# A new end for a decoder layer: gathered tokens settled per column group, folded part by products at the very end

## The chip, the cores and the metric

One NeuronCore of a Trainium2 chip. The metric is device time in microseconds (us) of one execution. TensorE (PE), VectorE (DVE), ScalarE (ACT), GpSimd (POOL) and SyncE (SP) each work through a list of instructions of their own, in order, and wait for each other by semaphores.

## What is computed

A decoder layer on 512 tokens of 2048 columns: a mixer, then an expert network (PEER) that picks 128 of 16384 single-neuron experts for every token. Only the end of the expert part is touched:

```
def apply(args):
    xb, ib, gb = args
    u = jnp.take(expert_u, ib, axis=0)
    a = jnp.einsum('thkd,td->thk', u, xb)
    w = (jax.nn.gelu(a.astype(jnp.float32), approximate=False) * gb).astype(xb.dtype)
    vv = jnp.take(expert_v, ib, axis=0)
    return jnp.einsum('thk,thkd->td', w, vv)
...
x = x + gate2[:, None, :] * ffn
```

All in float32.

## The kernel before

Of the 512 tokens, 352 are **dense**: every expert is computed for them, by products over all 16384 rows of `expert_u` and `expert_v`, with weights that are zero where an expert was not picked. The other 160 are **gathered**: the rows of their picked experts are fetched by indirect DMAs from POOL, and DVE multiplies and adds. The gathered tokens come in two groups: the first has 128 tokens, one on each partition. The second has 32 tokens, each of them on four partitions that hold a quarter of its experts each; its sum has to be folded, four partitions into one.

*Dense part.* The experts go in 16 chunks of 8 blocks of 128. For a chunk, `u_block` (L790) makes the activations of each block, `w_block` makes from them the weights `W`, and `v_group(ch, dg)` multiplies them with `expert_v` for four column groups `dg` of 512 columns (L943). Weights come by SP's queue (`vr`, L933, three buffers), and are split in two halves of fewer bits each (`split`, L88 on ACT for the upper half, L89 on DVE for the lower one); three products of 128x128 by 128x352 then stand for one of float32. A group of a chunk takes four loads of two blocks, each with 24 products: 96 products a group, 384 a chunk. In the last chunk the result of a group does not go to `acc`, but to `xs[dg]`: x from DRAM (`begin`, L966) plus `acc` times the gate (L970), plus the last chunk's sums times the gate (L951). `xs[dg]` is kept transposed: 128 columns on the partitions, tokens along the free dimension; tokens 0 to 127 are the first gathered group, 128 to 159 the second, 160 to 511 the dense ones.

*Gathered part.* `gathered` fetches 128 half rows of 1024 columns by one indirect DMA (L842, four buffers `gt`), and DVE adds each, times its weight, to `gacc` (L867). When the first group's sum is finished it goes to DRAM (`a_dram`), and the second group uses `gacc` again. In the last chunk all steps left are written into the program at once (`gather_to(NK)`), before the four calls of `v_group`; the last gathers are those of the second group's `expert_v`.

*The end.* In the last chunk `add_gathered(dg)` follows `v_group(dg)`, and `store` follows one group later (`ADD_AT`, `STORE_AT`). `add_gathered` loads the group's columns of `a_dram` (L976), transposes four blocks of them (L982) and four blocks of `gacc` (L986), copies both by ACT (L984, L987), folds the second by three additions on DVE each (L989), and corrects `xs` by both at once (L991). `store` transposes a whole group back, four tiles of 128 tokens (L1000), copies each (`ot`, L1003 on DVE, L1005 on ACT), and sends it to `out` (L1006).

*What sets the order.* The engines' lists are made by a scheduler of the framework, from the order of the source and an estimate of its own; so calls that follow each other in the source are interleaved. PSUM holds two buffers `pa` for transposes and three double buffers `pv`, which the sums of a group (two of them) and the transposes of `store` share.

Of the kernel before, what the change touches and what calls it, by code (L numbers as in the profile page):

```python
# [22 lines left out]
P = 128  # L23
# [23 lines left out]
ADD_AT = ((0,), (1,), (2,), (3,))  # L47
STORE_AT = ((), (0,), (1,), (2, 3))
# [30 lines left out]
def hymba_peer(tc, x, c, positions, w_ada, b_ada, norm1_g, w_in, conv_w, q_norm_g, k_norm_g,  # L79
# [18 lines left out]
    with ExitStack() as ctx:  # L98
# [9 lines left out]
        make_identity(nc, ident)  # L108
        modc = const.tile([P, 6, KC], F32, name="modc")
# [863 lines left out]
        def add_gathered(dg):  # L973
            if NG == 2:
                ar = fin.tile([P, 512], F32, name="ar")
                nc.sync.dma_start(ar, a_dram[:, dg * 512:(dg + 1) * 512])  # L976
            else:
                ar = gacc[:, dg * 512:(dg + 1) * 512]
            for j in range(4):
                k = dg * 4 + j  # L980
                pt = psA.tile([P, T], F32, name="pa").rearrange("p (j t) -> p j t", t=P)
                nc.tensor.transpose(pt[:, 0], ar[:, j * P:(j + 1) * P], ident)  # L982
                ft = fin.tile([P, TG], F32, name="ft")
                nc.scalar.activation(ft[:, 0:P], pt[:, 0], AF.Copy)  # L984
                if NG == 2:
                    nc.tensor.transpose(pt[:, 1], gacc[:, k * P:(k + 1) * P], ident)  # L986
                    nc.scalar.activation(ft[:, P:], pt[:, 1, 0:nb], AF.Copy)  # L987
                    for f in range(1, fold):
                        nc.vector.tensor_tensor(out=ft[:, P:], in0=ft[:, P:],  # L989
                                                in1=pt[:, 1, f * nb:(f + 1) * nb], op=OP.add)  # L990
                nc.vector.scalar_tensor_tensor(xs[dg][:, j, 0:TG], ft, modc[:, 5, k:k + 1], xs[dg][:, j, 0:TG],  # L991
                                               op0=OP.mult, op1=OP.add)

        def store(dg):
            for i in range(NT):
                if i % 2 == 0:
                    pq = psV.tile([P, 2, T], F32, name="pv")
                po = pq[:, i % 2]
# [3 lines left out]
                if i % 2:  # L1002
                    nc.vector.tensor_copy(ot, po)  # L1003
                else:
                    nc.scalar.activation(ot, po, AF.Copy)  # L1005
                nc.sync.dma_start(out[i * P:(i + 1) * P, dg * 512:(dg + 1) * 512], ot)  # L1006

# [45 lines left out]
```

## Time and profile before

| | us |
|---|---|
| median of 3 runs | 3570.03 |
| lowest, highest | 3550.63, 3575.09 |
| profiled execution | 3566.93 |
| its span, first to last instruction | 3565.0 |
| PE busy (share of the span) | 3243.3 (91%) |
| DVE busy | 2853.7 (80%) |
| POOL busy | 1403.5 (39%) |
| ACT busy | 1222.7 (34%) |

Times in the rows below are us from the span's start unless marked ns. A row of the timeline merges instructions of one kind that follow each other (`x44`); in brackets stands how long the engine had been idle before it, and what ended that. PEclk is the granted clock of TensorE as a share of 2.4 GHz. DMA is the mean busy share of the 16 DMA engines.

### The profile page before, as it was taken

The numbers are of one execution on the slowest core, as the hardware profiler recorded it, in microseconds if no ns is written. First come the engines' busy times: TensorE is split into PE (matmuls) and PEld (weight loads), VectorE is DVE, ScalarE is ACT, GpSimd is POOL, SyncE is SP. The second block draws the span as 40 slices with busy tenths as digits, with TensorE's granted clock in tenths as the row PEclk, the third lists the DMA queues.
The fourth block names the chain that finished last, engine by engine and source line by source line (L and its number), as shares of the span: only waits on it lengthen the run. The fifth ranks groups of instructions, "written<-read, shape, count | busy, mean of one in ns | idle before, by whom it ended". The sixth has DMA issues, their size and how long they took to land.

```text
span 3565.0 us, 48376 instructions
## 1 busy us (share of the span) xinstructions
PE 3243.3 (91%) x18006; PEld 2980.4 (84%) x18006; DVE 2853.7 (80%) x4261; ACT 1222.7 (34%) x1828; POOL 1403.5 (39%) x985
## 2 busy tenths in 40 slices
PE   5988999999998797899999989899999999999986
PEld 4766777777787696899899989899999999989985
DVE  5789776743369989778888888898988999988985
ACT  5232333342264357322232222233322233223222
POOL 2446332254346410135444343343343444334441
PEclk9999999999999899999999999999999999999998
DMA  8864755559722135899999999999999999999994
GB/s 284 284 226 149 253 192 182 183 167 314 219 74 79 60 141 190 245 302 303 300 305 303 290 306 312 299 297 301 306 305 301 292 315 312 303 291 295 298 304 171
DMA packets 417514, 896.26 MB, mean 251 GB/s; under 512 B 32209, under 2 KB 110974, under 8 KB 412542
## 3 DMA queue, kind: packets, MB, share of 16 engines
q1 hardware_dynamic: 325118, 557.59, 53.5%
q0 software_dynamic: 92160, 335.59, 27.8%
q8 instruction: 141, 2.31, 0.3%
q14 instruction: 95, 0.78, 0.1%
HBM read 843.47 MB, written 49.55 MB: 250 GB/s over the span
## 4 chain that ended last, share of the span: by engine, by line
DMA 39%; DVE 28%; PE 16%; issue 11%; POOL 3%; ACT 1%; SPq 1%; DVEq 0%; POOLq 0%; ACTq 0%
DMA gt<-in_expert_v_dram,idxu 10%; DMA gt<-in_expert_u_dram,idxu 7%; DMA vr<-in_expert_v_dram 4%; PE pm L457 4%; DMA ada_w<-in_w_ada_dram 4%; POOL gt L842 3%; DVE gacc L867 3%; DMA gt<-in_expert_v_dram,ib 3%; DVE ada_acc L196 2%; DMA ur<-in_expert_u_dram 2%; DVE utf L778 2%; DVE gt L851 2%; DMA gt<-in_expert_u_dram,ib 2%; DVE gt L905 2%; DVE vs L89 2%
## 5 line engine op out<-in xcount | busy, mean ns | idle before, releaser
L790 PE MATMUL pa<-hd,ut 128*128 128x352 f32 x6144 | 1084.3, 329 | 69.4 <-DVE ut L89 59.8
L943 PE MATMUL pv<-W,vs 128*128 128x352 f32 x6144 | 1081.3, 329 | 71.6 <-DVE vs L89 42.8
L943 PEld LDWEIGHTS pv<-W,vs 128*128 128x128 f32 x6144 | 1017.6, 192 | 89.5 <-DVE vs L89 54.0
L790 PEld LDWEIGHTS pa<-hd,ut 128*128 128x128 f32 x6144 | 1020.4, 192 | 82.2 <-DVE ut L89 70.1
L89 POOL TENSOR_TENSOR wsp<-wraw,wsp 128x1024 fp32r<-128x1024 f32 x160 | 392.8, 2457 | 565.5 <-ACT wsp L88 536.2
L842 POOL DMA_INDIRECT gt<-in_expert_u_dram,idxu x256 | 344.1, 1344 | 636.3 <-DVE gt L851 307.2
L88 ACT ACTIVATE vs<-vr 128x1024 fp32r<-128x1024 f32 x256 | 271.2, 1059 | 813.8 <-PE pv L943 384.8
L842 POOL DMA_INDIRECT gt<-in_expert_v_dram,idxu x256 | 329.2, 1286 | 493.4 <-DVE gacc L867 333.7
L867 DVE SCALAR_TENSOR_TENSOR gacc<-gt,ga_a,gacc 128x1024 f32<-128x1024 f32 x316 | 400.1, 1275 | 106.9 <-DMA gt<-in_expert_v_dram,idxu 74.9
L851 DVE SCALAR_TENSOR_TENSOR gt<-gt,h2n 128x1024 f32<-128x1024 f32 x320 | 385.5, 1216 | 123.3 <-DMA gt<-in_expert_u_dram,idxu 99.7
L88 ACT ACTIVATE ut<-utf 128x1024 fp32r<-128x1024 f32 x232 | 244.6, 1056 | 284.6 <-DVE utf L778 158.5
L89 DVE TENSOR_TENSOR vs<-vr,vs 128x1024 fp32r<-128x1024 f32 x256 | 309.2, 1209 | 37.2 <-ACT vs L88 37.2
L778 DVE STREAM_TRANSPOSE utf<-ur 128x1024 f32<-128x1024 f32 x232 | 286.7, 1237 | 6.7 <-issue 3.3
L88 ACT ACTIVATE wsp<-wraw 128x1024 fp32r<-128x1024 f32 x160 | 169.1, 1058 | 355.7 <-issue 94.1
L89 DVE TENSOR_TENSOR ut<-utf,ut 128x1024 fp32r<-128x1024 f32 x232 | 281.5, 1215 | 9.7 <-ACT ut L88 9.7
L457 PE MATMUL pm<-big,wsp 128*128 128x512 f32 x1152 | 285.6, 400 | 0.0
L457 PEld LDWEIGHTS pm<-big,wsp 128*128 128x128 f32 x1152 | 213.9, 191 | 42.2
L196 DVE SCALAR_TENSOR_TENSOR ada_acc<-ada_w,scol,ada_acc 128x512 f32<-128x512 f32 x195 | 211.5, 1085 | 28.0 <-DMA ada_w<-in_w_ada_dram 24.3
L245 PE MATMUL pqk<-wsp,big 128*128 128x512 f32 x768 | 193.1, 411 | 18.8 <-DVE qk L291 11.4
L699 PE MATMUL pm<-big,wsp 128*128 128x512 f32 x768 | 187.8, 402 | 17.0 <-POOL wsp L89 15.4
L245 PEld LDWEIGHTS pqk<-wsp,big 128*128 128x128 f32 x768 | 150.0, 198 | 55.5 <-DVE qk L291 14.2
L545 PE MATMUL pm<-big,wsp 128*128 128x512 f32 x768 | 182.7, 398 | 8.4 <-DVE x L551 8.4
(274 smaller groups left out, 3167.6 us busy)
## 6 DMA issues: line engine op xcount, KB each, us to landing
vr<-in_expert_v_dram SPq DMA_DIRECT2D x256, 512.0 KB
ur<-in_expert_u_dram SPq DMA_DIRECT2D x464, 256.0 KB
ada_w<-in_w_ada_dram SPq DMA_DIRECT2D x192, 512.0 KB
wraw<-in_w_in_dram SPq DMA_DIRECT2D x96, 512.0 KB
g_dram<-gtile SPq DMA_DIRECT2D x11, 2048.0 KB
g<-g_dram SPq DMA_DIRECT2D x32, 704.0 KB
wraw<-in_w_out_dram SPq DMA_DIRECT2D x32, 512.0 KB
wraw<-in_w_peer_q_dram SPq DMA_DIRECT2D x32, 512.0 KB
```

The source lines that it names most:

```text
L88: hi = nc.scalar.activation(dst[:, 0], src, AF.Copy)
L89: (eng or nc.vector).tensor_tensor(out=dst[:, 1], in0=src, in1=dst[:, 0].bitcast(F32), op=OP.subtract)
L196: nc.vector.scalar_tensor_tensor(new, wt[:, k], s, old, op0=OP.mult, op1=OP.add)
L245: nc.tensor.matmul(banks[i], hT[kk][:, a, i * P:(i + 1) * P], ws[:, b, k], start=(kk == last[0] and n == 0), stop=(kk == last[1] and n == 2))
L457: nc.tensor.matmul(banks[n2], ws[:, a, k, n2 * P:(n2 + 1) * P], hT[kk][:, b], start=(kk == 0 and n == 0), stop=(kk == KC - 1 and n == 2))
L699: nc.tensor.matmul(banks[j], ws[:, a, k, j * P:(j + 1) * P], h2T[kk][:, b], start=(kk == 0 and n == 0), stop=(kk == KC - 1 and n == 2))
L778: nc.vector.transpose(t, UR[0][:, :, q * 256:(q + 1) * 256].rearrange("p b (c r) -> p c b r", r=32))
L790: mm = nc.tensor.matmul(pa[:, :TD], ut[:, a, j], hd[k][:, b], start=(k == 0 and n == 0), stop=(k == KC - 1 and n == 2))
L842: d = nc.gpsimd.indirect_dma_start(out=t, out_offset=None, in_=src, in_offset=bass.IndirectOffsetOnAxis(ap=gidx[g][:, j:j + 1], axis=0), e ...
L851: nc.vector.scalar_tensor_tensor(t, t, 1.0, h2n[:, f * D // 2:(f + 1) * D // 2], op0=OP.mult, op1=OP.mult, accum_out=ga_a[:, f, j:j + 1])
L867: nc.vector.scalar_tensor_tensor(gacc[:, s], t, a, gacc[:, s], op0=OP.mult, op1=OP.add)
L943: mm = nc.tensor.matmul(pv[j // 2][:, j % 2, :TD], vs[:, a, bb, j * P:(j + 1) * P], W[e0 // 2][:, m, bb], start=(b == 0 and n == 0), stop= ...
```

## The change

`add_gathered` and `store(dg)` go; three functions come. `settle(dg)`, called one group late, corrects the tokens of the first gathered group alone, straight from PSUM (L996), and stores the three tiles that hold none of the second group's tokens: tiles 2, 3 and 0. `settle_last` follows everything: sixteen products of `gacc` with a 128x32 matrix of ones and zeros (`foldm`, made at the start from the identity by one DVE reduction) transpose and fold at once (L1004); one multiplication by the gate (L1007), an addition to each group (L1010), and tile 1 of each group is stored. The products are held behind the dense ones by an order without a wait.

```
-ADD_AT = ((0,), (1,), (2,), (3,))
-STORE_AT = ((), (0,), (1,), (2, 3))
...
+        foldm = const.tile([P, TG - P], F32, name="foldm")
+        nc.vector.tensor_reduce(foldm, ident.rearrange("p (f t) -> p t f", t=TG - P), axis=AX.X, op=OP.add)
...
-        def add_gathered(dg):
...
+        def store(dg, tiles):
+            for n, i in enumerate(tiles):
+                if n % 2 == 0:
                     pq = psV.tile([P, 2, T], F32, name="pv")
+                po = pq[:, n % 2]
...
+                if (n + dg) % 2:
                     nc.vector.tensor_copy(ot, po)
                 else:
                     nc.scalar.activation(ot, po, AF.Copy)
                 nc.sync.dma_start(out[i * P:(i + 1) * P, dg * 512:(dg + 1) * 512], ot)
+
+        def settle(dg):
+            ar = fin.tile([P, 512], F32, name="ar")
+            nc.sync.dma_start(ar, a_dram[:, dg * 512:(dg + 1) * 512])
+            pt = psA.tile([P, T], F32, name="pa").rearrange("p (j t) -> p j t", t=P)
+            for j in range(4):
+                nc.tensor.transpose(pt[:, j], ar[:, j * P:(j + 1) * P], ident)
+            for j in range(4):
+                k = dg * 4 + j
+                nc.vector.scalar_tensor_tensor(xs[dg][:, j, 0:P], pt[:, j], modc[:, 5, k:k + 1], xs[dg][:, j, 0:P],
+                                               op0=OP.mult, op1=OP.add)
+            store(dg, (2, 3, 0))
+
+        def settle_last():
+            pt = psA.tile([P, T], F32, name="pa").rearrange("p (k t) -> p k t", t=nb)
+            for k in range(KC):
+                mm = nc.tensor.matmul(pt[:, k], gacc[:, k * P:(k + 1) * P], foldm, start=True, stop=True)
+                tc.add_manual_dep(mm.ins, pace[-1].ins.name, ORDER, reason="products of the dense tokens first")
+            ft = fin.tile([P, KC, nb], F32, name="ft", bufs=1)
+            nc.vector.tensor_tensor(out=ft, in0=pt, in1=modc[:, 5, :, None].to_broadcast([P, KC, nb]), op=OP.mult)
+            for dg in range(4):
+                x_ = xs[dg][:, :, P:TG]
+                nc.vector.tensor_tensor(out=x_, in0=x_, in1=ft[:, dg * 4:dg * 4 + 4], op=OP.add)
+                store(dg, (1,))
...
-                if ch == nch - 1:
-                    for f in ADD_AT[dg]:
-                        add_gathered(f)
-                    for f in STORE_AT[dg]:
-                        store(f)
+                if ch == nch - 1 and dg:
+                    settle(dg - 1)
+        settle(3)
+        settle_last()
```

Line numbers of the split are two lower after the change (L86, L87). Up to the products of the last chunk the engines' lists are otherwise the same.

PE's list, from the last product of the first column group on, before the change (`pv` are the sums, `ar` the first gathered group, `gacc` the second, `xs` what is stored):

```order
L943 MATMUL pv<-W,vs 128x352 x36
L982 MATMUL pa<-ident,ar 128x128 x2
L943 MATMUL pv<-W,vs 128x352 x84
L986 MATMUL pa<-ident,gacc 128x128 x2
L982 MATMUL pa<-ident,ar 128x128 x2
L1000 MATMUL pv<-ident,xs 128x128 x5
L943 MATMUL pv<-W,vs 128x352 x14
```

and after it:

```order
L943 MATMUL pv<-W,vs 128x352 x52
L993 MATMUL pa<-ident,ar 128x128 x4
L943 MATMUL pv<-W,vs 128x352 x20
L979 MATMUL pv<-ident,xs 128x128 x2
L943 MATMUL pv<-W,vs 128x352 x4
L979 MATMUL pv<-ident,xs 128x128 x2
L993 MATMUL pa<-ident,ar 128x128 x4
L943 MATMUL pv<-W,vs 128x352 x24
L979 MATMUL pv<-ident,xs 128x128 x4
L993 MATMUL pa<-ident,ar 128x128 x4
L943 MATMUL pv<-W,vs 128x352 x20
L979 MATMUL pv<-ident,xs 128x128 x4
```

The transposes of `gacc` (L986), which stood behind 84 products of the second group and ahead of the 192 of the third and fourth, are gone from this place; transposes of stored tiles (L979) stand there, tile 0 last. The end of PE's list after the change:

```order
L943 MATMUL pv<-W,vs 128x352 x20
L1004 MATMUL pa<-foldm,gacc 128x32 x7
L979 MATMUL pv<-ident,xs 128x128
L1004 MATMUL pa<-foldm,gacc 128x32
L979 MATMUL pv<-ident,xs 128x128 x5
L1004 MATMUL pa<-foldm,gacc 128x32 x2
L979 MATMUL pv<-ident,xs 128x128
```

The products with `foldm` follow the last dense product, with transposes of the last group's tiles among them; 28 transposes of stored tiles stand behind the last dense product.

DVE's list before, from the second group's x on (`vs` is a split, `gacc` a gathered row added):

```order
L970 SCALAR_TENSOR_TENSOR xs<-acc,modc,xs 128x352 x4
L867 SCALAR_TENSOR_TENSOR gacc<-gt,ga_a,gacc 128x1024 x7
L989 TENSOR_TENSOR ft<-ft,pa 128x32 x6
L991 SCALAR_TENSOR_TENSOR xs<-ft,modc,xs 128x160 x2
```

These rows close the gathers before the change, with six splits still behind them. After the change, from the copy of a stored tile of the first group on:

```order
L867 SCALAR_TENSOR_TENSOR gacc<-gt,ga_a,gacc 128x1024 x2
L982 COPY ot<-pv 128x512
L87 TENSOR_TENSOR vs<-vr,vs 128x1024
L951 SCALAR_TENSOR_TENSOR xs<-pv,modc,xs 128x352 x4
L970 SCALAR_TENSOR_TENSOR xs<-acc,modc,xs 128x352 x4
L996 SCALAR_TENSOR_TENSOR xs<-pa,modc,xs 128x128 x4
L87 TENSOR_TENSOR vs<-vr,vs 128x1024
L867 SCALAR_TENSOR_TENSOR gacc<-gt,ga_a,gacc 128x1024 x2
L982 COPY ot<-pv 128x512
L87 TENSOR_TENSOR vs<-vr,vs 128x1024
```

The last gathers are spread between splits, copies and corrections, and reach to two splits before the end of the dense part. On SP six stores of the first two groups stand between the loads of the last weights, one ahead of each of the last six; before the change four stood in a row ahead of the last three.

## Rows read from the trace of the kernel before

**Rows 1.** The page's head.

```profile
span 3565.0 us, 48376 instructions
```

**Rows 2.** Busy time of each engine by stretch of the tail.

```profile
core 0: us, PE busy (x) PEld busy (x) DVE busy (x) ACT busy (x) POOL busy (x), PEclk, DMA share, GB/s
...
3467.00:3488.00 21.00, 18.18 (x86) 17.18 (x84) 13.66 (x17) 4.56 (x6) 7.32 (x5) 0.79 0.71 256
...
3488.00:3508.00 20.00, 0.11 (x1) 0.11 (x2) 14.72 (x18) 0.16 (x1) 7.51 (x5) 0.54 0.68 248
...
3508.00:3553.00 45.00, 41.04 (x254) 39.04 (x255) 24.52 (x70) 12.41 (x34) 0.00 (x0) 0.94 0.35 117
...
3556.00:3558.00 2.00, 0.82 (x7) 0.56 (x5) 1.32 (x8) 0.81 (x4) 0.00 (x0) 1.00 0.69 252
```

**Rows 3.** Waits from 3455 us on: total, times, longest.

```profile
PE pa L986 <- DVE gacc L867: 20.8, 1, 20.8
...
DVE gacc L867 <- DMA gt<-in_expert_v_dram,ib: 14.0, 6, 4.2
...
DVE vs L89 <- ACT vs L88: 8.9, 4, 4.1
```

**Rows 4.** Timeline of the tail: start, duration, engine, line, operation.

```profile
3466.77 1.06 DVE L951 SCALAR_TENSOR_TENSOR xs<-pv,modc,xs 128x352 f32<-128x352 f32 x2
...
3476.07 2.88 POOL L842 DMA_INDIRECT gt<-in_expert_v_dram,ib  x1 [10.33 <-DVE gacc L867]
...
3478.19 8.88 PE L943 MATMUL pv<-W,vs 128*128 128x352 f32 x44 [1.89 <-DVE vs L89]
...
3485.35 1.28 DVE L867 SCALAR_TENSOR_TENSOR gacc<-gt,ga_a,gacc 128x1024 f32<-128x1024 f32 x1 [3.69 <-DMA gt<-in_expert_v_dram,ib]
...
3487.70 1.28 DVE L867 SCALAR_TENSOR_TENSOR gacc<-gt,ga_a,gacc 128x1024 f32<-128x1024 f32 x1 [1.06 <-DMA gt<-in_expert_v_dram,ib]
...
3507.89 0.69 PE L986 MATMUL pa<-ident,gacc 128*128 128x128 f32 x2 [20.82 <-DVE gacc L867]
...
3544.63 7.93 PE L943 MATMUL pv<-W,vs 128*128 128x352 f32 x48
...
3560.44 1.29 DVE L1003 COPY ot<-pv 128x512 f32<-128x512 f32 x2 [1.87 <-ACT ot L1005]
```

**Rows 5.** Groups by shape from 3455 us on: busy us, mean ns, idle before.

```profile
L867 DVE SCALAR_TENSOR_TENSOR gacc<-gt,ga_a,gacc 128x1024 f32<-128x1024 f32 x17 | 21.3, 1281 | 14.0 <-DMA gt<-in_expert_v_dram,ib 14.0
...
L89 DVE TENSOR_TENSOR vs<-vr,vs 128x1024 fp32r<-128x1024 f32 x11 | 13.4, 1220 | 8.9 <-ACT vs L88 8.9
...
L951 DVE SCALAR_TENSOR_TENSOR xs<-pv,modc,xs 128x352 f32<-128x352 f32 x16 | 8.4, 574 | 3.5 <-PE pv L943 3.5
...
L970 DVE SCALAR_TENSOR_TENSOR xs<-acc,modc,xs 128x352 f32<-128x352 f32 x16 | 8.3, 578 | 5.0 <-DMA xs<-x_dram 5.0
...
L1000 PE MATMUL pv<-ident,xs 128*128 128x128 f32 x64 | 10.9, 292 | 3.9 <-DVE xs L991 1.5 <-DVE xs L951 1.4 <-ACT ot L1005 0.9
...
L1003 DVE COPY ot<-pv 128x512 f32<-128x512 f32 x8 | 5.4, 686 | 2.1 <-ACT ot L1005 1.9
...
L991 DVE SCALAR_TENSOR_TENSOR xs<-ft,modc,xs 128x160 f32<-128x160 f32 x16 | 5.5, 382 | 0.1
```

**Rows 6.** The same view over the whole span, plain float products.

```profile
L914 PE MATMUL pv<-og,gt 128*128 128x128 f32 x704 | 99.4, 288 | 24.2 <-DVE og L908 24.2
```

**Rows 7.** PE by stretch: length, busy (instructions), PEclk, DMA share, GB/s.

```profile
3469.00:3472.00 3.00, 3.00 (x12) 0.50 1.02 391
...
3478.00:3481.00 3.00, 2.81 (x12) 0.71 0.56 121
...
3481.00:3484.00 3.00, 3.00 (x15) 0.72 0.94 320
```

**Rows 8.** Chain that ended last: one x load; SP's timeline: three weight loads.

```profile
3456.18 16.33 DMA xs<-x_dram
...
3481.69 11.93 SPq L933 DMA_DIRECT2D vr<-in_expert_v_dram  x3
```

More of the change, by code (lines that the diff above doesn't have):

```diff
@@ L971, in begin @@
                                                op0=OP.mult, op1=OP.add)
-        def add_gathered(dg):
[L974 to L996, printed above, removed]
+        def store(dg, tiles):
+            for n, i in enumerate(tiles):
+                if n % 2 == 0:
                     pq = psV.tile([P, 2, T], F32, name="pv")
-                po = pq[:, i % 2]
+                po = pq[:, n % 2]
                 for j in range(4):
@@ L1001, in store @@
                 ot = fin.tile([P, T], F32, name="ot", bufs=4)
-                if i % 2:
+                if (n + dg) % 2:
                     nc.vector.tensor_copy(ot, po)
```

## The prediction

> **What bounds the kernel now.** I read the page first, then only the last 112 us, since the diff touches nothing earlier but one small reduction at the start. The profiled execution spans 3565.0 us [rows 1] and took 3566.9 us, so 1.9 us lie around its span; it stands 3.1 us under the median of the runs, 3570.0 us. All sums below are against this execution; 3.1 us are added at the end.
>
> The table by stretch shows where the tail's time goes: TensorE (PE) is busy 18.18 of 21 us up to 3488, 0.11 of the next 20 us, then 41.04 of 45 us [rows 2]; what follows is output. The waits name the hole: PE stood 20.8 us, once, at the transposes of the gathered sum (L986) until VectorE (DVE) had finished it (L867) [rows 3]. The timeline gives the ends: the second column group's products end at 3487.07 (3478.19 + 8.88), PE goes on at 3507.89, the last product ends at 3552.56, the last copy at 3561.73, and 3.3 us later the span ends [rows 4]. Behind that wait, in PE's order, stood 192 of the 384 products of the last chunk; they take 44.7 us (3507.89 to 3552.56). At the pace of the last 48 (7.93 us, 0.165 us each) they need 31.7 us [rows 4].
>
> **The change, part by part.** I number the seventeen gathers that DVE adds after the last weight block G1 to G17 (17 of 1.28 us each [rows 5]), and the split weights of the last chunk 0 to 15.
>
> *The start.* One DVE reduction from the identity: DVE has nothing to do there, it waits for the first loads. Cost zero; uncovered it would be below 1 us.
>
> *Up to the end of the second group's products.* Up to the last weight block all orders are the same, and the first group's sums still wait for the same x load: 3466.77 [rows 4]. Two things then come sooner. Eight transposes of the first group's stored tiles and twelve of the gathered sum's stored part stand between the products; four corrections of xs (L996) stand ahead of split 6 on DVE. A correction is 128x128; the nearest row, 128x160, takes 0.38 us [rows 5], so 1.4 us for four. Against it the second x load no longer follows a 256 KB load, worth some 0.5 us. So split 6, for which PE waits in the row at 3478.19, comes 0.9 us later. Of the twenty transposes, twelve fall into this wait; eight follow, at 0.17 us (10.9 us for 64 [rows 5]) 1.4 us. If the clock does better than in that row (44 products in 8.88 us, 7.3 us at 0.165) 1.6 us come back. Range +0.4 to +2.3 us; I take **+1.5 us**.
>
> *The wait removed.* PE's order has no product behind the gathered sum any more; L1004 stands behind them all. **-20.8 us.** What is late next: the transposes of tile 0 (first group), which wait for a DVE copy that stands behind G9 and G10. Their gathers are issued as before, when G5 and G6 are done (GpSimd's queue holds gathers alone, in the same order); G9, issued at 3476.07, arrived at 3485.35, G10 at 3487.70 [rows 4]. So G10 ends near 3489, the copy (0.69 us [rows 5]) and split 8 (1.22 us) near 3491: PE stands about 2 us there. Split 9 then comes behind four sums of 0.57, four x additions of 0.58, four corrections and split: some 7 us after split 8, while PE needs about 5 us for the 24 products and eight transposes between: a second gap of 2 us.
>
> *The 192 products.* 31.7 us of products, 32 transposes among them at 0.17, 5.4 us, the two gaps, 4.0 us. After such a gap of 1.9 us (PE's wait for split 6) the granted clock was 0.71 and 0.72 in two stretches of 3 us [rows 7]: 12 and 15 products where 17.0 and 18.2 would go at 0.165 us, 8.2 x 0.165 = 1.4 us. Two gaps: 2.8 us. Sum 43.9 us where 44.7 stood: **-0.8 us**. DVE has, in this stretch, nine gathers (11.5), eight splits (9.8), two sets of sums and two of x additions (9.2), two sets of corrections (2.8) and four copies (2.7): 36.0 of 43.9 us. It is nearly as full as PE, which is why the gaps stay. Bounds: with no gap and full clock 37.1 us (6.8 less); the upper ones are rivals below.
>
> *SyncE's queue.* Stores now stand ahead of weight loads 10 to 15, and each waits for its copy. Load 10 leaves about 1 us later than the first of the three issued from 3481.69 [rows 8]; DVE wants it near 3501. The slowest landing that I read is the x load's 16.33 us [rows 8], so it fits, as do the later ones, each issued 10 to 18 us ahead. Nothing is charged. If a landing exceeds its lead, the excess goes straight into PE's path.
>
> *The end.* Removed from here: the last additions of folded parts and their ScalarE copies, and four transposes each of the two gathered parts. The stores that remain are about as many, 28 transposes after the last product against 30. Added after the last product: sixteen products with the fold matrix. None is in the trace; the nearest is the plain 128x128 float product L914, 352 of them (two records each) in 99.4 us, 0.28 us each [rows 6]; the lower bound is a transpose, 0.17. I take 0.28 since it is the same kind: 4.5 us (2.7 at least). With eight transposes of the last group among them, 1.4; the multiplication of 128x512 and a copy, 0.7 each; four additions of at most 0.38, 1.5 in all; the last group's transposes and its copy, 0.7 each: 10.2 us, where before 9.2 us lie between last product and last copy [rows 4]. **+1.0 us** (-0.8 at the lower bound). The 3.3 us of the last store stay.
>
> Sum: 1.5 - 20.8 - 0.8 + 1.0 = -19.1 us. 3566.9 - 19.1 = 3547.8 us for an execution like the profiled one; 3551 us against the median. I predict **3550 us**.
>
> **Rivals.**
> *Everything is covered:* no gap, full clock, cheap fold products: 6.8 + 1.8 + 1.1 us more, -28.8 us, 3541 us. For it: DVE's 36.0 us are less than PE's. Against it: the two engines wait for each other in a fixed order.
> *Half clock.* While PE ran after the idle stretch before 3467, twelve products filled 3.00 us at a granted 0.50 [rows 7], the 1.2 GHz level, 0.25 us each. If the gaps and the transposes keep the clock there for the 192, it costs 192 x 0.085 = 16.3 us, less the 2.8 already charged: -5.6 us, 3564 us. Against it: between 3556 and 3558, where PE did transposes alone and only 0.82 of 2 us, the clock was 1.00 [rows 2]. The Trainium skill, TensorE: Matmul & The Clock Gate, Part 4: PE-mode transpose, says that transposes do not count as TensorE activity for the clock gate. That stretch does not show a fall of the clock under them; by the rule the 3564 us of this rival would be the forecast.
> *DVE's waits stay.* In before DVE waited 14.0 us for gathered rows and 8.9 us for ScalarE's halves [rows 3]. If those come in addition to 36.0 us, the stretch takes 58.9 instead of 43.9 us: -4.1 us, 3566 us. For it: gathers and splits are now interleaved on one in-order engine. Against: nine of the gathers now stand 10 us or more after their issue.
> *Slower.* G9, G13 and G17 each open a round of four buffers. In the walk they have 9.3, 14.7 and 14 us from issue to use. With a landing of L each, the delay is (L - 9.3) + (L - 14.7) + (L - 14); at 16.3 us it is 10.9, at about 19 us it eats all the gain, at 24.5 (half more than the slowest row) it is 35.5: 3586 us. For it: 16 stores of 256 KB now share the DMA engines with the gathers. Against: between 3488 and 3508 these moved only part of the time, 0.68 [rows 2].
>
> **How the numbers follow.** The forecast 0.62 (3543 to 3558), all covered 0.12, half clock 0.11, DVE's waits 0.11, slower 0.04. The runs of before lie between 3550.6 and 3575.1 us, 24.5 us or 0.7% apart, so 1%, 35.7 us, is about what a measurement of this kernel can tell from no change. Of the cases none reaches 1% by itself; the covered one with a low run does: faster 0.12, within 1% 0.85, slower 0.03. The range 3530 to 3567 holds the first four cases but the edges, and leaves out the slower one and a low run of the covered one.
>
> **What would show it.** Right: no wait of PE for L867 over 3 us before the last product; last product near 3533 us; L1004 near 4.5 us; from last product to last copy about 10 us. Wrong: granted clock 0.5 over more than two stretches of 3 us between 3488 and 3533; a wait of DVE for gathered rows over 6 us behind G10; PE waiting for weights' loads; the first 3455 us differing by more than the runs do.

## The result and the profile after

The changed kernel is slower: 3593.42 us median (3579.66 to 3612.11, 10 runs) against 3568.03 us for the kernel before (3550.63 to 3579.33, 10 runs) on the same chip. The ratio is 1.0084, with a 95% interval of 1.0065 to 1.0103: 0.84%, or 30 us by the ratio. The forecast was 3550 us, about 20 us faster.

The page's head answers to [rows 1]; it is 22.6 us longer.

```profile
span 3587.6 us, 48297 instructions
```

The first thing to look for is where the two traces part. The weights `W` give marks that both have: the first row of DVE that multiplies one by its scores, and the split of the last `W`, which is the last step of the dense part ahead of the final chunk's products. The two marks in DVE's timeline of the kernel before (start, duration, line, operation):

```profile
1450.13 1.69 DVE L822 TENSOR_TENSOR W<-W,g 128x704 f32<-128x704 f32 x2
...
3454.20 0.88 DVE L89 TENSOR_TENSOR W<-ge,W 128x704 fp32r<-128x704 f32 x1
```

and the same two marks in the changed kernel:

```profile
1444.39 1.69 DVE L822 TENSOR_TENSOR W<-W,g 128x704 f32<-128x704 f32 x2 [0.17 <-DMA g<-g_dram]
...
3498.55 0.88 DVE L87 TENSOR_TENSOR W<-ge,W 128x704 fp32r<-128x704 f32 x1
```

At the first mark the changed kernel is 5.7 us ahead; at the last it is 44.4 us behind. What lies between, called the **loop** from here on, took 2004.1 us (3454.20 - 1450.13) and now takes 2054.2. This is a stretch in which the change moves no instruction: the engines' lists are the same there, step for step. From the last `W` to the end of the span it is the other way round: 3565.0 - 3455.08 = 109.9 us before, 3587.6 - 3499.43 = 88.2 us after, 21.7 us less. (The stretch from the last `W` on takes 107.9 to 113.1 us in the twelve kernels of this study that have the old end, and 87.8 to 89.6 in the five that have the new one.) The new end does what was forecast (19.1 us less), and 50 us are lost where nothing was changed.

The tail after, TensorE's (PE) timeline with four rows of DVE:

```profile
3512.92 4.47 PE L943 MATMUL pv<-W,vs 128*128 128x352 f32 x14 [5.40 <-DVE xs L951]
...
3527.87 3.46 PE L943 MATMUL pv<-W,vs 128*128 128x352 f32 x20
...
3538.33 1.11 PE L993 MATMUL pa<-ident,ar 128*128 128x128 f32 x4 [6.43 <-DMA ar<-a_dram]
...
3570.85 3.44 PE L943 MATMUL pv<-W,vs 128*128 128x352 f32 x20
...
3574.14 1.64 PE L1004 MATMUL pa<-foldm,gacc 128*128 128x32 f32 x14
...
3578.52 0.69 DVE L1007 TENSOR_TENSOR ft<-pa,modc 128x512 f32<-128x512 f32 x1
...
3579.72 0.89 DVE L1010 TENSOR_TENSOR xs<-xs,ft 128x128 f32<-128x128 f32 x4
...
3583.72 0.69 DVE L982 COPY ot<-pv 128x512 f32<-128x512 f32 x1 [0.99 <-PE pv L979]
```

The 20.8 us for `gacc` [rows 3] are gone. The second group's products end at 3531.33, the last product at 3574.29, the last copy at 3584.41.

The loop's own views show what became slower. Its middle by stretch, the kernel before (columns: length, busy time of each engine, granted clock, DMA share, GB/s):

```profile
core 0: us, PE busy (x) PEld busy (x) DVE busy (x) ACT busy (x) POOL busy (x), PEclk, DMA share, GB/s
1600.00:3200.00 1600.00, 1508.91 (x9085) 1486.47 (x9084) 1403.60 (x1518) 467.56 (x523) 668.71 (x507) 0.98 1.01 303
```

and the changed kernel:

```profile
1600.00:3200.00 1600.00, 1485.71 (x8846) 1462.37 (x8844) 1364.55 (x1467) 454.22 (x509) 642.09 (x492) 0.97 1.02 295
```

The DMA engines are full in both (shares of 1.01 and 1.02), but they move 303 GB/s before and 295 after: 2.6% less, and in the same 1600 us PE gets 2.6% fewer instructions done (8846 against 9085). So it looks as if the loads set the pace in this stretch and became slower; the experiments below test that. The groups by line of the same stretch say the same of DVE (busy, mean ns of one, idle before and what ended it). Before:

```profile
L851 DVE SCALAR_TENSOR_TENSOR gt<-gt,h2n 128x1024 f32<-128x1024 f32 x251 | 301.8, 1215 | 91.7 <-DMA gt<-in_expert_u_dram,idxu 81.9 <-DMA gt<-in_expert_u_dram,ib 7.8 <-issue 1.8
L778 DVE STREAM_TRANSPOSE utf<-ur 128x1024 f32<-128x1024 f32 x190 | 235.0, 1237 | 5.6 <-issue 3.3 <-DMA ur<-in_expert_u_dram 1.6 <-DVE gacc L867 0.7
```

After:

```profile
L851 DVE SCALAR_TENSOR_TENSOR gt<-gt,h2n 128x1024 f32<-128x1024 f32 x236 | 283.9, 1215 | 103.1 <-DMA gt<-in_expert_u_dram,idxu 101.5 <-DMA gt<-in_expert_u_dram,ib 1.5
L778 DVE STREAM_TRANSPOSE utf<-ur 128x1024 f32<-128x1024 f32 x184 | 227.6, 1237 | 21.9 <-DMA ur<-in_expert_u_dram 17.7 <-issue 4.1 <-DVE ge L822 0.2
```

One instruction takes as long as before (1215 and 1237 ns); the waits ahead of it grew, and a DMA ends them (81.9 to 101.5 us and 1.6 to 17.7 us).

What can make the same loads slower? In the compiled program nothing of them differs but the place they write to. The new constant tile `foldm` takes 128 bytes of every partition at the low ("left") end of SBUF, and every tile that is placed above it on that side moves up by 128 bytes. In the loop these are `gt` (the gathered rows; 25600 to 25728), `ur` (raw blocks of `expert_u`, L510; 71168 to 71296), `g4` (the scores that L822 multiplies, loaded from `g_dram`, L817; 112128 to 112256), the split weights `W`, the sum `gacc`, and the tiles made from `ur`. All of these lay on multiples of 512 bytes and lie 128 bytes past one now. The raw weights `vr` stand on the right side of SBUF and keep their place (145120, which is 224 past a multiple of 256).

### The profile page after: what moved, and what is told of

Same layout as the page of the kernel before. It is cut to its first block, busy times and chain, and to the rows that moved or that the text cites. A ratio compares the mean times of both kernels' runs of the same rounds, so it can differ in the third digit from the quotient of the medians.

```text
span 3587.6 us, 48297 instructions
## 1 busy us (share of the span) xinstructions
PE 3259.0 (91%) x18022; PEld 2996.4 (84%) x18022; DVE 2847.7 (79%) x4219; ACT 1216.3 (34%) x1796; POOL 1396.3 (39%) x985
## 4 chain that ended last, share of the span: by engine, by line
DMA 36%; DVE 26%; PE 19%; issue 13%; POOL 5%; SPq 1%; ACT 1%; DVEq 0%; POOLq 0%; ACTq 0%
DMA gt<-in_expert_v_dram,idxu 9%; DMA gt<-in_expert_u_dram,idxu 8%; DMA ur<-in_expert_u_dram 5%; PE pm L457 4%; PE pv L943 4%; PE pa L790 4%; DMA ada_w<-in_w_ada_dram 3%; POOL gt L842 3%; DMA vr<-in_expert_v_dram 3%; DVE utf L778 2%; DVE gt L905 2%; DVE gt L851 2%; DVE ut L87 2%; DVE gacc L867 2%; DMA gt<-in_expert_u_dram,ib 2%
## 5 line engine op out<-in xcount | busy, mean ns | idle before, releaser
L87 POOL TENSOR_TENSOR wsp<-wraw,wsp 128x1024 fp32r<-128x1024 f32 x160 | 393.2, 2460 | 560.0 <-ACT wsp L86 540.4
L86 ACT ACTIVATE vs<-vr 128x1024 fp32r<-128x1024 f32 x256 | 271.2, 1059 | 884.1 <-DMA vr<-in_expert_v_dram 442.3
L851 DVE SCALAR_TENSOR_TENSOR gt<-gt,h2n 128x1024 f32<-128x1024 f32 x320 | 385.4, 1215 | 140.7 <-DMA gt<-in_expert_u_dram,idxu 118.7
L86 ACT ACTIVATE ut<-utf 128x1024 fp32r<-128x1024 f32 x232 | 244.2, 1056 | 289.8 <-DVE utf L778 184.8
L87 DVE TENSOR_TENSOR vs<-vr,vs 128x1024 fp32r<-128x1024 f32 x256 | 309.0, 1208 | 35.2 <-ACT vs L86 34.8
L778 DVE STREAM_TRANSPOSE utf<-ur 128x1024 f32<-128x1024 f32 x232 | 286.7, 1237 | 22.2 <-DMA ur<-in_expert_u_dram 17.9
L86 ACT ACTIVATE wsp<-wraw 128x1024 fp32r<-128x1024 f32 x160 | 169.1, 1058 | 364.2 <-issue 92.1
L87 DVE TENSOR_TENSOR ut<-utf,ut 128x1024 fp32r<-128x1024 f32 x232 | 281.5, 1215 | 12.3 <-ACT ut L86 12.2
L457 PE MATMUL pm<-big,wsp 128*128 128x512 f32 x1152 | 286.9, 401 | 0.0
L457 PEld LDWEIGHTS pm<-big,wsp 128*128 128x128 f32 x1152 | 214.6, 191 | 42.5 <-issue 0.2
L699 PE MATMUL pm<-big,wsp 128*128 128x512 f32 x768 | 189.3, 404 | 15.1 <-POOL wsp L87 13.4
L699 PEld LDWEIGHTS pm<-big,wsp 128*128 128x128 f32 x768 | 147.0, 195 | 48.0 <-POOL wsp L87 16.1
```

The source lines that it names most:

```text
L86: hi = nc.scalar.activation(dst[:, 0], src, AF.Copy)
L87: (eng or nc.vector).tensor_tensor(out=dst[:, 1], in0=src, in1=dst[:, 0].bitcast(F32), op=OP.subtract)
L457: nc.tensor.matmul(banks[n2], ws[:, a, k, n2 * P:(n2 + 1) * P], hT[kk][:, b], start=(kk == 0 and n == 0), stop=(kk == KC - 1 and n == 2))
L699: nc.tensor.matmul(banks[j], ws[:, a, k, j * P:(j + 1) * P], h2T[kk][:, b], start=(kk == 0 and n == 0), stop=(kk == KC - 1 and n == 2))
L778: nc.vector.transpose(t, UR[0][:, :, q * 256:(q + 1) * 256].rearrange("p b (c r) -> p c b r", r=32))
L851: nc.vector.scalar_tensor_tensor(t, t, 1.0, h2n[:, f * D // 2:(f + 1) * D // 2], op0=OP.mult, op1=OP.mult, accum_out=ga_a[:, f, j:j + 1])
```

## The experiments

Theory A: the loads write more slowly to the new places. Rival B: the new end, or the new stores, cost the loop its time. Rival C: the reduction itself. Rival D: any shift, or any new program, costs about as much. Each run has as its measure the ratio to the kernel before on the same chip, and from its profiled execution the loop (first to last `W`) and the tail (end of the last `W` to the end of the span). The expectations of the first three runs count the loop from the first split of a `W`, some 90 us later: their 1913.7 and 1964.7 us are the 2004.1 and 2054.2 us here.

### The tile alone, in the kernel before

The old end is kept; nothing reads the tile.

```
+        foldm = const.tile([P, TG - P], F32, name="foldm")
+        nc.vector.tensor_reduce(foldm, ident.rearrange("p (f t) -> p t f", t=TG - P), axis=AX.X, op=OP.add)
         modc = const.tile([P, 6, KC], F32, name="modc")
```

> The kernel before plus one constant tile of 128 bytes per partition and the one VectorE reduction that fills it; nothing reads it, and the old end is kept. In the program every later tile of the left side of SBUF starts 128 bytes higher, so the destinations of the gathered expert rows (gt, ur) move from multiples of 512 bytes to 128 past one. Theory A (placement: the loads of the main loop land more slowly at these places): the main loop from the first to the last weight block gets about 50 us longer, as in the changed kernel (1913.7 against 1964.7 us), the end stays at about 110 us, some 3605 to 3620 us in all where before takes 3568. Rival B (the loss comes from the new end, or from the stores in SyncE's queue): no difference from before, 3568 within 8 us. Rival C (the reduction itself): also no difference, since it is one instruction of under 1 us at the start.

Measured: 3619.45 us, ratio 1.0128 (1.0096 to 1.0160); loop 2055.2 us, tail 110.2. The stretch in the loop's middle:

```profile
1600.00:3200.00 1600.00, 1483.35 (x8830) 1458.60 (x8829) 1360.94 (x1461) 451.09 (x506) 651.19 (x489) 0.97 1.02 294
```

The whole loss is there with the old end in place: 2055.2 us for the loop where the changed kernel has 2054.2, and 294 GB/s. B falls.

### The same tile in 512 bytes, in the kernel before

```
+        foldp = const.tile([P, P], F32, name="foldp")
+        foldm = foldp[:, 0:TG - P]
+        nc.vector.tensor_reduce(foldm, ident.rearrange("p (f t) -> p t f", t=TG - P), axis=AX.X, op=OP.add)
```

> As the kernel before plus the same reduction, but the tile takes 512 bytes per partition, of which the reduction fills the first 128. All later tiles of the left side move by 512 bytes and so lie on multiples of 512 bytes again. Theory A (placement against 512-byte multiples, or a smaller power of two above 128): as before, 3568 within 8 us, main loop near 1914 us. Rival D (any shift of the tiles, or any change of the program, costs): as the run with 128 bytes, about 3610 us. Rival C (the reduction itself): the same loss in both.

Measured: 3567.78 us, ratio 0.9992 (0.9971 to 1.0013); loop 2001.3 us. The stretch:

```profile
1600.00:3200.00 1600.00, 1510.75 (x9079) 1489.35 (x9078) 1401.78 (x1513) 465.46 (x522) 669.66 (x505) 0.98 1.01 302
```

The same reduction, into a tile that takes 512 bytes, and no loss: C and D fall.

### The changed kernel with its tile in 512 bytes

```
-        foldm = const.tile([P, TG - P], F32, name="foldm")
+        foldp = const.tile([P, P], F32, name="foldp")
+        foldm = foldp[:, 0:TG - P]
```

> The changed kernel with its fold matrix in a tile of 512 bytes per partition, of which it uses the first 128; nothing else differs. Theory A: main loop back to about 1914 us, end at about 88 us as in the changed kernel, so 3568 - 21 = about 3547 us (3540 to 3555). Rival B (the new end costs the main loop its time in some way): about 3593 us, as the changed kernel. Rival D: about 3593 us too.

Measured: 3544.06 us (3541.52 to 3556.59), ratio 0.9928 (0.9910 to 0.9946); loop 2003.3 us, tail 89.6. With one tile padded the change is 0.72% faster than before, some 26 us. The groups by line of the loop's middle, beside those above:

```profile
L852 DVE SCALAR_TENSOR_TENSOR gt<-gt,h2n 128x1024 f32<-128x1024 f32 x249 | 299.6, 1217 | 93.4 <-DMA gt<-in_expert_u_dram,idxu 84.7 <-DMA gt<-in_expert_u_dram,ib 8.3
L779 DVE STREAM_TRANSPOSE utf<-ur 128x1024 f32<-128x1024 f32 x189 | 234.2, 1240 | 9.0 <-DMA ur<-in_expert_u_dram 5.5 <-issue 3.5
```

The waits that DMAs end are back near those of the kernel before (84.7 and 5.5 us).

### vr aligned as well

```
+        vpad_p = ctx.enter_context(tc.tile_pool(name="vpad_p", bufs=1, side="right"))
+        vpad = vpad_p.tile([P, 56], F32, name="vpad")
+        nc.gpsimd.memset(vpad, 0.0)
         vp = ctx.enter_context(tc.tile_pool(name="vp", bufs=2, side="right"))
```

> The changed kernel with the 512-byte fold tile and besides a pad of 224 bytes per partition on the right side of SBUF, ahead of the tiles of the down weights (vr, vs) and their sums: the loads of vr then start on a multiple of 512 bytes, where in all other runs they start 224 bytes past one. Theory A, if it is a matter of every DMA destination: some 10 to 40 us below the run with the 512-byte tile alone, since vr brings about half as many bytes as the gathered expert rows of the main loop. If only the places of gt and ur matter, or vr is not what the main loop waits for: the same as the run with the 512-byte tile alone, about 3547 us, within 5.

Measured: 3537.83 us (3529.67 to 3541.77), ratio 0.9907 (0.9892 to 0.9922); loop 1999.1 us, tail 87.8. The intervals of this run and the one before it overlap, and the loop differs by 4 us: what `vr`'s place is worth is at most a fraction of what the other tiles' places are.

### Which of the tiles: gt or the expert blocks

For `gt`, the 128-byte tile and, ahead of the pool of the expert blocks (`up`), a pad of 384 bytes; for the blocks, only a pad of 128 bytes there:

```
+        pad_p = ctx.enter_context(tc.tile_pool(name="pad_p", bufs=1))
+        pad = pad_p.tile([P, 96], F32, name="pad")    # 32 columns in the second run
+        nc.gpsimd.memset(pad, 0.0)
         up_ctx = ctx.enter_context(ExitStack())
```

> The kernel before with the 128-byte tile and its reduction, as in the run with 128 bytes, and a pad of 384 bytes per partition between the tiles of the gate weights W and those of the expert blocks: the gathered rows (gt) land 128 bytes past a multiple of 512, the expert blocks (ur, the score tiles g4) on a multiple again. If each packet that starts off the multiple costs the same extra (the gathers have some 82,000 packets of 4 KB, the expert blocks 59,000 of 2 KB and the scores 45,000 of 512 bytes), about 0.44 of the 46 to 50 us: some 3590 us. If only the gathers matter: about 3618. If only the expert blocks and scores matter: as before, about 3569.

> The other half: the kernel before with a pad of 128 bytes per partition between W and the tiles of the expert blocks, and no other change: ur and g4 land 128 bytes past a multiple of 512, gt on a multiple. By an equal cost per packet about 0.56 of the 46 to 50 us: some 3596 us. If only the gathers matter: as before, about 3569; if only these matter: about 3618.

Measured: with `gt` (and `W` and `gacc`) moved 3589.85 us, ratio 1.0059 (1.0033 to 1.0085), loop 2025.1; with `ur` and `g4` moved 3594.86 us, ratio 1.0067 (1.0036 to 1.0098), loop 2032.9. Each is a part, and the two add up to the whole (0.59 + 0.67 against 1.28%). That fits an equal cost per packet, but later runs show that this was chance.

### Which offsets

The same tile with 256, 32, 64 and 224 bytes, in the kernel before:

```
-        foldm = const.tile([P, 32], F32, name="foldm")
+        foldm = const.tile([P, 64], F32, name="foldm")    # 8, 16 and 56 columns in the others
```

> As the run with 128 bytes, with a tile of 256 bytes: gt, ur and g4 land on odd multiples of 256 bytes. If the loss comes from packets that start off a multiple of 256: as before, about 3569 us. If it needs a multiple of 512: about 3618 us. If the loss grows with the distance from the multiple: above 3618.

> As the run with 128 bytes, with a tile of 32 bytes: gt, ur and g4 land 32 bytes past a multiple of 512. If each packet off the multiple costs one more access, whatever its offset: about 3618 us. If the cost is the bytes between the multiple below and the start, which are moved for nothing: a quarter of the loss, about 3581 us. If only larger offsets matter: 3569.

> As the run with 128 bytes, with a tile of 64 bytes: gt, ur and g4 land 64 bytes past a multiple of 256. The 32-byte tile cost more (2.1%) than the 128-byte one (1.3%), which neither a fixed cost per packet nor the bytes from the multiple below explain. If a place that is no multiple of 64 costs something of its own: as the 128-byte run, some 3612 us. If the cost falls steadily as the offset grows from 32 to 128: between them, some 3628 us. If it is the bytes after all and the 32-byte run had another cause: 3589 us.

> As the run with 128 bytes, with a tile of 224 bytes: gt, ur and g4 land 224 bytes past a multiple of 256, where vr lies in the kernel before. If only the power of two matters that divides the place (32, as in the 32-byte run): some 3642 us. If the cost falls as the offset grows, 32 costing most: below the 128-byte run, some 3590 us. If it grows with the bytes between the multiple below and the start: 7/4 of the loss at 128, about 3647 us, the same as by the power of two, which this run can't part from it.

Measured, with the runs above for comparison:

| `gt`, `ur`, `g4` past a multiple of 512 by | median us | ratio (95% interval) | loop us |
|---|---|---|---|
| 0 (before) | 3568.03 | 1 | 2004.1 |
| 0 (tile of 512 bytes) | 3567.78 | 0.9992 (0.9971 to 1.0013) | 2001.3 |
| 256 | 3568.72 | 1.0004 (0.9979 to 1.0028) | 2004.6 |
| 128 | 3619.45 | 1.0128 (1.0096 to 1.0160) | 2055.2 |
| 64 | 3625.58 | 1.0177 (1.0147 to 1.0207) | 2061.6 |
| 32 | 3644.41 | 1.0213 (1.0166 to 1.0260) | 2081.4 |
| 224 | 3635.56 | 1.0193 (1.0152 to 1.0234) | 2087.6 |

A multiple of 256 is enough. Off it, each of the four places tried costs 1.3% or more, and 128 costs least. A cost that grows with the bytes between the multiple below and the start would put 32 lowest; one that falls as the offset grows would put 224 lowest; both fall. The power of two that divides the place would order the rows as they stand (32 and 224 alike, then 64, then 128), but the intervals of 32, 64 and 224 overlap, so the order among these three is not shown. The 32-byte run's middle of the loop has the lowest rate but one (224 bytes: 290 GB/s):

```profile
1600.00:3200.00 1600.00, 1468.22 (x8770) 1441.39 (x8769) 1355.15 (x1452) 449.51 (x502) 638.12 (x487) 0.97 1.02 292
```

The Trainium skill, in DMA: Bandwidth & Descriptors, How a descriptor splits into AXI transactions, says that the first access of a descriptor that does not start on a multiple of 256 bytes starts at the multiple below. It speaks of bytes that are fetched; the places that these runs move are the ones written. The boundary that it names is the one that these runs show (256 free, 128 not). Its count of bytes does not give the costs; an estimate worked out from that page: 512 bytes from an offset of 32 need 17 beats of 32 bytes, from 128 need 20 and from 224 need 23, where 16 are needed on the boundary, so 32 would cost least; here 32 costs 2.13% and 128 costs 1.28%.

### Every load aligned, and an earlier load of the gathered sum

A tile of 32 bytes ahead of the first phase's big tiles and a pad of 224 bytes as the first tile of the right side put `ada_w`, `wraw` and `vr` on multiples of 256 too:

```
+        epad = early.tile([P, 8], F32, name="epad")
+        nc.gpsimd.memset(epad, 0.0)
...
+        rpad_p = ctx.enter_context(tc.tile_pool(name="rpad_p", bufs=1, side="right"))
+        rpad = rpad_p.tile([P, 56], F32, name="rpad")
+        nc.gpsimd.memset(rpad, 0.0)
         gw_ctx = ctx.enter_context(ExitStack())
```

> The changed kernel with the 512-byte fold tile, a 32-byte tile in front of the big tiles of the first phase and a 224-byte pad as the first tile of the right side: beside gt, ur and g4 now also the loads of the first phase (the modulation weights ada_w, 100 MB; wraw, 84 MB) and vr start on multiples of 256, which in the kernel before lie 224 past one. If every load that starts off a multiple costs time where the DMA engines are full (the main loop, the first 180 us or so): 5 to 15 us below the run with vr alone aligned, some 3525 to 3533 us. If only the main loop's loads matter: as that run, 3538 us.

Measured: 3532.67 us (3521.47 to 3547.07), ratio 0.9916 (0.9886 to 0.9946). That is the same as the run with only `vr` aligned besides (0.9907); the first `W` comes at 1437.9 us there, against 1440.0. The 185 MB of the first phase gave nothing that can be seen. Of the expected 5 to 15 us the upper part is ruled out; a gain of a few us would be lost in intervals this wide.

On top of it, the load of `ar` moved from `settle` to `begin`:

```
         tc.add_manual_dep(t.ins, behind.ins.name, ORDER, reason="weights first")
+        ars[dg] = fin.tile([P, 512], F32, name="ar", bufs=3)
+        nc.sync.dma_start(ars[dg], a_dram[:, dg * 512:(dg + 1) * 512])
```

> The run before this one, and the gathered sum's stored parts (ar) are loaded together with the x tiles (xs) of their group, ahead of the weights that follow, instead of behind the stores of the group before (three buffers). In the changed kernel TensorE waits 6.4 us for the last of them. If that wait is on the path: 4 to 6 us less than without it. If VectorE, which is nearly as full there, is late in its place: no difference.

Measured: 3524.68 us (3507.97 to 3546.54), ratio 0.9891 (0.9854 to 0.9929); tail 82.8 us against 87.9. This is the fastest kernel of the study by its median, 1.1% under the kernel before; against the run without the early load the intervals overlap. In the profile PE's wait of 6.5 us for the last `ar` is gone. PE's timeline of this run has two rows for the first two `ar`:

```profile
3449.55 1.09 PE L1000 MATMUL pa<-ident,ar 128*128 128x128 f32 x4 [5.72 <-issue]
...
3455.05 0.66 PE L1000 MATMUL pa<-ident,ar 128*128 128x128 f32 x4 [0.54 <-DMA ar<-a_dram]
```

The 5.72 us stand where the run without it waited 6.0 us for DVE's `xs`; that gap stayed, and only the other one went.

### Are W or vr part of it?

The run that moved `gt` moved `W` too, which no load writes and PE reads. And `vr` had given back so little that it was put 128 bytes off:

```
+        wpad_p = ctx.enter_context(tc.tile_pool(name="wpad_p", bufs=1))
+        wpad = wpad_p.tile([P, 32], F32, name="wpad")
+        nc.gpsimd.memset(wpad, 0.0)
         wpool = ctx.enter_context(tc.tile_pool(name="wpool", bufs=NW))
... (and a pad of 384 bytes behind it)

-        vpad = vpad_p.tile([P, 56], F32, name="vpad")
+        vpad = vpad_p.tile([P, 24], F32, name="vpad")
```

> The kernel before with a pad of 128 bytes per partition ahead of the split gate weights W and one of 384 behind them: only W, which ScalarE and VectorE write and TensorE reads, lies 128 bytes past a multiple of 256; gt, ur and g4 keep their places modulo 512. If it is the destinations of the loads: as before, the loop from the first to the last W at about 2004 us. If it is the operands of the engines: part or all of the 21 us by which the run that moved gt and W together was longer, some 2025 us.

> The changed kernel with the 512-byte fold tile and a pad of 96 bytes on the right side: vr, vs and acc lie 128 bytes past a multiple of 256; gt, ur and g4 lie on one. At the cost per packet that gt, ur and g4 showed at 128 bytes (50 us for 186,000 packets) vr's 65,536 packets of 2 KB would make the loop some 17.6 us longer than with vr aligned (1999 us): about 2017 us, 3555 in all. If vr's place does not matter, as its 224 bytes suggest: 1999 to 2003 us, about 3540 in all.

Measured: `W` alone 3567.19 us, ratio 0.9983 (0.9962 to 1.0004): `W`'s place costs nothing that shows. The additions to `gacc`, which moved with `gt` too, take 1277 ns there against 1275 before. So the loss of the run with `gt` belongs to `gt`. (The loop of the profiled execution with `W` alone moved was 2020.6 us, though it began 11 us early: the loop of one execution scatters by as much as 16 us, and only the ratios decide differences of that size.) `vr` 128 bytes off: 3541.56 us, ratio 0.9921 (0.9898 to 0.9943), loop 1999.5. With an equal cost per packet the loop should have been 2017 us. None of the three places of `vr` that were tried (0, 128 and 224 past a multiple of 256) costs anything that shows.

### g4 or ur

```
                 if e % 4 == 0:
+                if e == 0:
+                    gpad = up.tile([P, 32], F32, name="gpad", bufs=1)
+                    nc.gpsimd.memset(gpad, 0.0)
                     G4[0] = up.tile([P, TD // GB, 4, GB], F32, name="g4", bufs=1)
```

For `ur` the pad of 128 bytes ahead of the pool, and 96 columns in `gpad`, which put `g4` on a multiple of 512 again.

> The kernel before with a pad of 128 bytes per partition ahead of the score tile g4 alone: its packets of 512 bytes land 128 bytes past a multiple of 256; gt and ur keep their places, and with g4 moves only ge, which no load writes. At an equal cost per packet g4 has 45,000 of the 104,000 packets that the run with ur and g4 moved: 0.43 of its 0.67%, 0.29%, some 3576 us. If the 512-byte packets carry all of it: 0.67%, 3590 us. If only ur mattered: as before, 3566.

> The other part: ur, and with it ut and utf, 128 bytes past a multiple of 256, and a second pad of 384 bytes that keeps g4 on one. At an equal cost per packet 0.57 of 0.67%: 0.38%, some 3580 us, and vr, whose packets are as long, is an exception. If packets of 2 KB are spared, as vr's: as before, 3566. If only ur mattered: 3590.

Measured: `g4` alone 3592.88 us, ratio 1.0075 (1.0053 to 1.0096); `ur` alone 3575.33 us, ratio 1.0017 (0.9995 to 1.0038). Only the ratios part the two: the loops of the profiled executions, 2018.6 and 2014.3 us, lie within the scatter of one execution. The scores, 23 MB in packets of 512 bytes, carry as much of the loss as the 336 MB of gathered rows, and the 122 MB of `ur` little or nothing. The three parts are 0.75, 0.59 and 0.17%, together 1.5%; the changed kernel against its padded form is 1.0084 / 0.9928 = 1.0157. So `vr` is no exception: direct loads with packets of 2 KB (`vr`, `ur`) are spared or nearly so, the direct load with packets of 512 bytes and the indirect one with 4 KB are not. The trace's packet records, grouped by size, show the scores' packets between 1600 and 2200 us:

| packets of 512 bytes | mean ns | ninth tenth ends at, ns |
|---|---|---|
| before | 28.0 | 27 |
| changed kernel | 30.0 | 35 |
| `g4` alone moved | 29.6 | 35 |
| `ur` alone moved | 27.5 | 27 |

The packets themselves get longer when `g4` is moved, and not when `ur` is. The 2 ns do not account for the loss by themselves: 45,056 such packets on 16 engines make 5.6 us, where 0.75% are 27 us. DVE does not wait for the scores either: it was idle for 0.0 us ahead of the multiplication by them (between 1600 and 3200 us), before and with `g4` moved. For the gathers' packets one execution does not settle it: their mean in those 1600 us was 192.6 ns before and 196.7 with `gt` moved, but also 195.8 with `W` alone moved, which lost nothing. How the rest comes about, and why the gathers pay and `vr` doesn't, stays open.

## Why the prediction was wrong

**The step that failed** stands in two sentences of it: the reduction at the start, "Cost zero; uncovered it would be below 1 us", and "Up to the last weight block all orders are the same". Both are true of instructions: the run with the tile in 512 bytes has the same reduction and costs nothing that shows, and the lists are the same. But the argument read only time and order. A new tile in a constant pool also takes a place, and every later tile of that side moves by its size; 128 bytes is the one thing about `foldm` that mattered, and it was in the diff: `TG - P` columns of four bytes. The tiles that moved cost the loop 50 us (2004.1 to 2054.2); with the new tile padded it took 2003.3. The row that could have raised the question stands on the page of the kernel before, which the prediction used for its head alone: the busy share of the DMA engines in 40 equal slices, in tenths. From 1515 us to the last slice but one it is 9 without a break:

```profile
DMA  8864755559722135899999999999999999999994
```

The prediction's own list of what would show it wrong had the right item ("the first 3455 us differing by more than the runs do"): 44.4 us at the last `W`.

**The tail** went by the steps, against the last `W`:

- *Up to the end of the second group's products:* +1.5 us forecast; 3487.07 - 3455.08 = 32.0 us before, 3531.33 - 3499.43 = 31.9 after, so -0.1, below the range of +0.4 to +2.3. The later split 6 that was charged does not show: where PE waited 1.89 us for it before [rows 4], it runs on after its 5.40 us for `xs` without a gap until 3531.90.
- *The wait removed:* -20.8 us, right. What is late next was named wrongly: not the copy behind G10 and not split 9, twice 2 us, but once 6.43 us for the last of the four loads of `ar`. SyncE's timeline (start, time to issue) has it behind a load of x and the first store of a tile:

```profile
3524.10 0.45 SPq L985 DMA_DIRECT2D out_dram<-ot  x1
...
3524.65 0.37 SPq L990 DMA_DIRECT2D ar<-a_dram  x1
```

  It could not have gone much sooner: `ar` has two buffers, and PE read the one that this load fills until 3523.22. PE goes on at 3538.33, 13.7 us after the issue. The walk asked of the weights whether they land in time, and charged this load nothing. Moving it ahead, with a third buffer, takes some 5 us off the tail (87.9 to 82.8 in one execution each).
- *The 192 products:* 43.9 us forecast, 3574.29 - 3531.33 = 43.0 measured. That the sum agrees is partly luck, since another gap stands in it: 6.43 us once, where twice 2.0 were charged. After it the granted clock was 0.50 up to 3541, a cost that the forecast had charged: the first 28 products (3539.10 on) took 6.32 us, 1.7 more than at 0.165 us each, where 2.8 were charged for two gaps. The transposes cost less than charged: four of them among the products took 0.36 us (3549.53 to 3549.89) where 0.68 was charged. The stretches of the tail after, by their granted clock, and three smaller ones within the last:

```profile
3499.00:3531.00 32.00, 24.96 (x125) 24.07 (x126) 24.75 (x35) 4.84 (x5) 14.80 (x10) 0.75 0.82 281
3531.00:3575.00 44.00, 37.57 (x236) 36.98 (x234) 31.64 (x47) 9.59 (x11) 5.26 (x5) 0.92 0.67 247
...
3536.00:3541.00 5.00, 2.67 (x10) 2.67 (x11) 5.00 (x9) 0.00 (x0) 0.00 (x1) 0.50 1.04 412
3541.00:3543.00 2.00, 2.00 (x9) 2.00 (x9) 0.43 (x1) 0.00 (x0) 1.70 (x2) 0.61 1.00 384
3543.00:3575.00 32.00, 32.00 (x213) 31.86 (x211) 21.72 (x30) 8.05 (x9) 1.74 (x2) 1.00 0.53 187
```

  DVE is busy 31.64 us in the second, where the walk had 36.0 us of work for it; seven gathers were left for it instead of nine, which is 2.6 us of the difference.
- *The end:* 10.2 us forecast from last product to last copy, 3584.41 - 3574.29 = 10.1 measured; the products with the fold matrix 4.5 us forecast, and the group has 3.9:

```profile
L1004 PE MATMUL pa<-foldm,gacc 128*128 128x32 f32 x32 | 3.9, 263 | 0.0
```

  The last store is 3.2 us.
- Sum: -19.1 forecast, -21.7 in the two profiled executions. The padded form gives -0.72% (-0.54 to -0.90), 19 to 32 us. So the forecast of 3550 us fits the change without its 128 bytes, which took 3544.06 us.

**The rivals.** *Everything covered* (3541): nearer to the padded form than expected, but with a wait of 6.43 us that is not covered. *Half clock* (3564): after the 6.43 us without a product the granted clock fell to 0.50, the lower level, but from 3543 to 3575 it was 1.00, with 24 transposes among the products, so it did not stay there. The rule that the prediction named beside it (the Trainium skill, TensorE: Matmul & The Clock Gate, Part 4: PE-mode transpose) would have given this time; the trace of the changed kernel does not show its effect at this share of transposes. *DVE's waits stay* (3566): DVE waited 4.5 us for gathered rows after 3499, where it had been 14.0 [rows 3]. *Slower* (gathered rows land late): its sign came true and its mechanism did not; no wait for gathered rows over 3.7 us shows in the tail.

## What to carry to other kernels

A tile added to a pool that lives long moves every tile placed after it; when the loop behind it is bound by DMA, ask where the destinations of its loads now lie, and pad the new tile to a multiple of 256 bytes, so that places which lay on such a multiple stay on one. Here this decides the sign: the same change is 0.84% slower with 128 bytes and 0.72% faster with 512. When two traces differ, compare first the times of marks that both have, stage by stage; the loss may lie where the diff is silent.

## What was not expected of the hardware

In a stretch with the DMA engines full (shares of 1.01 to 1.02), destinations off a multiple of 256 bytes cost up to 4% of the rate (303 to 292 GB/s with 32 bytes and 290 with 224) and 1.3 to 2.1% of the whole time. Offsets of 32 and 224 cost more than 128, where the estimate above by a count of bytes has 32 lowest. Not all loads pay: 23 MB in packets of 512 bytes cost 0.75%, 336 MB of gathered rows in packets of 4 KB 0.59%; direct packets of 2 KB cost 0.17% with `ur` (122 MB), an interval that holds zero, and nothing that shows with `vr` (134 MB). Why these differ is open. And in the first phase, where the DMA engines are less full (a mean share of 0.58 up to 1450 us), moving 185 MB of loads onto multiples of 256 changed nothing that could be measured.
